# SSD output projection: seven products of quarters instead of eight, with the sums made by adding DMAs

## The chip, the cores and the metric

The kernel runs on one core of one Trainium2 chip. The metric is the device time of one execution in microseconds (us); less is better. The engines are TensorE (PE for its matmuls, PEld for its weight loads), VectorE (DVE), ScalarE (ACT), GpSimd (POOL) and SyncE (SP, which here only issues DMAs). Each has its own queue and works it off in order; semaphores join them.

## What is computed

One hybrid decoder layer on 1024 tokens of width 1024, in float32. Cut to what matters:

```python
h = rms_norm(x, norm_mix_g)
z, xbc, dt_raw, q_a, kv_a, k_rope_raw, gates = split(h @ w_in)
y_ssd = ssd_mixer(z, xbc, dt_raw, ...) @ w_ssd_proj     # (1024 x 2048) @ (2048 x 1024): the changed product
y_mla = mla_mixer(q_a, kv_a, k_rope_raw, ...) @ w_mla_proj
g_ssd, g_mla = split(sigmoid(gates + gate_b))
x = x + (g_ssd * y_ssd + g_mla * y_mla) @ w_o           # the merge, and w_o
h = rms_norm(x, norm_ffn_g)
x = x + ffn(h)                                          # gated MLP with a causal convolution

def ssd_mixer(z, xbc, dt_raw, ...):                     # state space scan: 4 groups of 8 heads, 8 chunks of 128 tokens
    xbc = silu(causal_depthwise_conv(xbc))
    y = ssd_chunked_scan(...) + xs * d_skip
    y = y * silu(z)
    return rms_norm(y in 4 groups of 512, norm_g)
```

## The kernel before

Activations lie with channels on the partitions and tokens along the row: a tile is 128 channels x 512 tokens (half the sequence). Precision is kept by splitting every operand in a high and a low part (`hi` is a rounding cast on ACT, `lo` the remainder on DVE or POOL); one step of a product is then three matmuls (`mm3`): hi x hi, hi x lo, lo x hi.

**The scan.** `ssd_steps(g)` goes through the 8 chunks of group g. Per chunk: transposes and scores on PE (tiles `xp`, `sp`), DVE's `sm`, `xdt`, `xde`, `bt`, `seg`, `abc` made from them, the new state (`sn` on PE, then `st`: multiplied by `cdec` on POOL, summed on DVE), and the output (`yp` on PE, added and gated on DVE into `xg`). Between these steps PE takes matmuls of other projections from a list, `background`: `conv_group(g + 1)`, which projects and convolves the next group's channels, `z_tiles`, and for the last group `mla_tiles`. Their tile is `lin`. `conv_group` gives way (`yield False`) as long as `finished[0] < g - 1`. `ssd_finish(g, half)` norms one half of a group: sums of squares and a Newton root on small tiles (`grr`, `rsa`), transposes into `np_`, four products on DVE (L957), and a store into `y_d` (L965). It is resumed a piece at a time from the loop over the next group, and its last act for half 1 is to set `finished[0]`.

**The projection.** The first half's y is split into `ya0` (from `y_d`, or directly for the last group). Then for each half and each of 8 column tiles, 16 tiles of k are multiplied into one PSUM bank: 8 x 2 x 16 x 3 = 768 matmuls of 128x512. The first of the 16 outputs begins inside the scan's last part (`first_ssd_tile`, the head). Behind each output come gates `gt` and the MLA part `mt` (loaded by POOL's queue) and the merge: (gt + 1) * y + mt, then half of it is split into `m`, all with DVE and ACT. Weights are loaded by SP in pieces of 256 KB into two buffers `wraw`, cast by ACT and subtracted by DVE (`whi`, `wlo`).

**w_o.** When the 8 merged tiles of a half are there, w_o follows, on top of x, loaded in one DMA of 2 MB per half into `x2` (L1240), then the FFN. Order: projection half 0, w_o half 0, projection half 1, w_o half 1. A framework orders each engine's queue by its own model of the program; in some stretches the order written in the code is kept.

Of the kernel before, what the change touches and what calls it, by code (L numbers as in the profile page):

```python
# [9 lines left out]
F32 = mybir.dt.float32  # L10
# [62 lines left out]
def tile_hybrid_layer(ctx: ExitStack, tc: tile.TileContext, x, cols, cons, w_main, w_small, w_uq, w_ukv,  # L73
# [15 lines left out]
    y_d = dram.tile([2 * D, T], F32, name="y_d")  # L89
# [83 lines left out]
    def mm3(ps, a, b, first, last, **more):  # L173
        (ah, al), (bh, bl) = a, b
        PE.matmul(ps, lhsT=ah, rhs=bh, start=first, stop=False, **more)  # L175
        PE.matmul(ps, lhsT=ah, rhs=bl, start=False, stop=False, **more)  # L176
        PE.matmul(ps, lhsT=al, rhs=bh, start=False, stop=last, **more)  # L177

# [163 lines left out]
    with tc.tile_pool(name="ap", bufs=2) as apool, tc.tile_pool(name="bls", bufs=4, space=PSUM) as bls:  # L342
# [48 lines left out]
        for half in range(2):  # L391
# [380 lines left out]
    with tc.tile_pool(name="dp", bufs=2) as dp, tc.tile_pool(name="psx", bufs=1, space=PSUM) as psx, \  # L772
# [166 lines left out]
        def ssd_finish(g, half):  # L939
# [16 lines left out]
            for j in range(4):  # L956
# [3 lines left out]
                if g == GROUPS - 1 and half == 0:  # L960
# [3 lines left out]
                else:  # L964
                    nc.sync.dma_start(out=y_d[r0:r0 + P, s], in_=x[:, j, s])  # L965
            if half:
# [27 lines left out]
        def mla_tiles():  # L994
# [11 lines left out]
            def y_step(j):  # L1006
# [5 lines left out]
                if j < 24 and j % 2 == 0:  # L1012
# [4 lines left out]
                    staged.append(raw_load(y_d, k, hs_(0), raw))  # L1017
# [34 lines left out]
        def first_ssd_tile():  # L1052
            ws = [load_w(w_ssd[0, kp], [P, KD, P]) for kp in range(2)]
            ps = lin_tile()
            head.append(ps)
            for k in range(16):
                while ya0[k] is None:
                    yield False
                hi, lo = ws[k // KD]
                mm3(ps, (hi[:, k % KD, :], lo[:, k % KD, :]), (ya0[k][:, 0, :], ya0[k][:, 1, :]), k == 0, k == 15)  # L1060
                yield True
# [40 lines left out]
        background.append(first_ssd_tile())  # L1102
# [70 lines left out]
    with tc.tile_pool(name="ep", bufs=2) as ep:  # L1173
        x2b = []
        with tc.tile_pool(name="em", bufs=2) as em:
# [32 lines left out]
            m0 = [em.tile([P, 2, 512], F32R, name="ma", bufs=3) for _ in range(3)]  # L1208
            for half in range(2):
                if half:  # L1210
                    w_raw(q0, loaded)
                    w_raw(q1, loaded)
                s = hs_(half)
                ya = ya0 if half == 0 else [load_act(y_d, k * P, s) for k in range(16)]
                ms = []
                for ct in range(8):
                    gt = em.tile([P, 512], F32, name="gt")
                    nc.gpsimd.dma_start(out=gt, in_=g_d[ct * P:(ct + 1) * P, s])
                    mt = em.tile([P, 512], F32, name="mt")
                    nc.gpsimd.dma_start(out=mt, in_=m_d[ct * P:(ct + 1) * P, s])  # L1220
                    if half == 0 and ct == 0:
                        ps = head[0]
                    else:
                        ps = lin_tile()
                        drain([steps([load_w(w_ssd[ct, kp], [P, KD, P]) for kp in range(2)], ya, ps, range(16), 16)])
                    if ct == 5:
                        loaded = last(mybir.EngineType.SP)
                    V.scalar_tensor_tensor(gt, gt, 1.0, ps, op0=ALU.add, op1=ALU.mult)
                    V.tensor_tensor(gt, gt, mt, op=ALU.add)  # L1229
                    m = em.tile([P, 2, 512], F32R, name="m", bufs=5) if ct >= 3 else \  # L1230
                        em.tile([P, 2, 512], F32R, name="ma", bufs=3) if half else m0[ct]
                    S.mul(m[:, 0, :], gt, 0.5)
                    V.scalar_tensor_tensor(m[:, 1, :], gt, 0.5, m[:, 0, :].bitcast(F32), op0=ALU.mult, op1=ALU.subtract)
                    ms.append(m)
                if half:
                    x0 = [x2b[0][:, i, :] for i in range(4)]
                    drain([norm(x0, x0, ep, x2ss[0])])
                big = ep.tile([P, 4, D], F32, name="x2")
                x2b.append(big)
                nc.sync.dma_start(out=big, in_=x[s, :].rearrange("(i p) c -> p i c", p=P))  # L1240
                behind(loaded)
                sq4 = ep.tile([P, 4, 2], F32, name="sq4")
                x2ss.append(sq4)
                nq = 0
                for ch in range(2):
                    banks = [bank6() for _ in range(4)]
                    qs = slice(ch * 512, (ch + 1) * 512)
                    for kp in range(4):
# [8 lines left out]
                        if half and (ch, kp) in ((1, 0), (1, 1)):  # L1257
                            q = pairs[kp]
                            q.a = w_split(q.r1, hp_tiles(), V)
                            w_sums(q, act_tile().rearrange("p a (b c) -> p (a b) c", c=P).bitcast(F32) if kp else None)  # L1260
                        if half and (ch, kp) == (1, 3):
# [5 lines left out]
                        for i in range(4):  # L1267
                            tk = slice(i * P, (i + 1) * P)
                            for k in range(2):
                                m = ms[2 * kp + k]  # L1270
                                mm3(banks[i], (m[:, 0, tk], m[:, 1, tk]), (wh[:, k, :], wl[:, k, :]),
                                    kp == 0 and k == 0, kp == 3 and k == 1)
                            if kp == 3:
                                V.tensor_tensor(big[:, i, qs], banks[i], big[:, i, qs], op=ALU.add)
                                junk = em.tile([P, 512], F32, name="junk", bufs=1)
# [4 lines left out]
                            if half and i % 2 and nq < KD:  # L1280
# [504 lines left out]
    for n, ins in enumerate(nc.cur_bb.bb.instructions):  # L1785
        if ins.engine == mybir.EngineType.PE or \
                (n < start_end or strict <= n < strict_end or n >= ordered) and ins.engine != mybir.EngineType.SP:
# [87 lines left out]
```

## Time and profile before

| | |
|---|---|
| runs (three) | 2176.78, 2179.0, 2181.62 us; median 2179.0 |
| profiled execution | 2178.96 us, its span 2177.1 us |
| granted TensorE clock, mean | 0.999 |
| POOL, share of the span | 41% |
| moved by DMA | 269.50 MB, mean 124 GB/s |
| scan with projections beside it | about 880 to 1260 us |
| projection half 0, then w_o half 0 | about 1260 to 1348, then from 1348 us |

The profile is of one execution. A busy PE is not PE at its peak: matmuls overlap, so the distance between starts tells more than a duration. In rows of groups, the idle time named is that of the engine just before the group's instructions, with what ended most of it.

### The profile page before, as it was taken

How to read it: one execution, taken by the hardware profiler on the slowest of the kernel's cores; microseconds unless marked ns; L12 is line 12 of the kernel's file. 1: busy time of each engine (PE TensorE's matmuls, PEld its weight loads, DVE VectorE, ACT ScalarE, POOL GpSimd, SP SyncE). 2: the span in 40 equal slices, each digit the busy share in tenths (PEclk: the TensorE clock that was granted, in tenths of full speed). 3: DMA queues.
4: the chain of work that ended last, by engine and by line, in shares of the span. 5: the costliest groups of instructions: out<-in, count | busy, mean ns of one | idle time of the engine just before them, and what ended most of it. 6: DMA issues, size and time to landing. Idle time of an engine off the chain costs nothing.

```text
span 2177.1 us, 30390 instructions
## 1 busy us (share of the span) xinstructions
PE 2136.6 (98%) x10844; PEld 1708.5 (78%) x10844; DVE 1445.6 (66%) x2613; ACT 1063.4 (49%) x2032; POOL 885.1 (41%) x1001
## 2 busy tenths in 40 slices
PE   8999999999999999999999999999999999999999
PEld 7877777777777887777878887888778888888887
DVE  4566656575665369898877755645786666677873
ACT  5445544555454446565654423324655554454441
POOL 2344424432542237665546411003098787750000
PEclk9999999999999999999999999999999999999999
DMA  4221111111211324645366557453132232348852
GB/s 149 70 68 43 44 55 58 52 40 55 65 40 64 121 75 137 193 155 179 105 203 208 167 193 252 163 189 102 63 121 100 99 101 98 112 150 315 275 188 83
DMA packets 121912, 269.50 MB, mean 124 GB/s; under 512 B 13536, under 2 KB 25760, under 8 KB 121760
## 3 DMA queue, kind: packets, MB, share of 16 engines
q1 hardware_dynamic: 105744, 214.99, 29.6%
q0 software_dynamic: 14528, 49.29, 6.7%
q10 hardware_dynamic: 1488, 3.28, 0.4%
q8 instruction: 85, 1.39, 0.3%
q14 instruction: 67, 0.55, 0.1%
HBM read 201.97 MB, written 65.54 MB: 123 GB/s over the span
## 4 chain that ended last, share of the span: by engine, by line
PE 75%; DVE 13%; ACT 5%; DMA 4%; issue 2%; POOL 1%; SPq 0%; ACTq 0%; DVEq 0%; POOLq 0%
PE lin L175 14%; PE lin L177 14%; PE lin L176 13%; PE dps L176 6%; PE dps L175 6%; PE dps L177 6%; PE pv L670 3%; PE s L175 2%; PE s L176 2%; PE s L177 2%; DVE xg L812 1%; PE s L627 1%; DMA wraw<-in_w_ssd 1%; PE yp L891 1%; PE s L610 1%
## 5 line engine op out<-in xcount | busy, mean ns | idle before, releaser
L175 PE MATMUL lin<-h,whi 128*128 128x512 f32 x1440 | 592.4, 411 | 2.2 <-DVE lt L330 2.2
L177 PE MATMUL lin<-h,wlo 128*128 128x512 f32 x1440 | 563.9, 392 | 0.0
L176 PE MATMUL lin<-h,whi 128*128 128x512 f32 x1440 | 562.9, 391 | 0.0
L175 PEld LDWEIGHTS lin<-h,whi 128*128 128x128 f32 x1440 | 271.0, 188 | 84.8 <-issue 33.8
L177 PEld LDWEIGHTS lin<-h,wlo 128*128 128x128 f32 x1440 | 270.6, 188 | 59.7
L176 PEld LDWEIGHTS lin<-h,whi 128*128 128x128 f32 x1440 | 271.7, 189 | 53.4 <-issue 7.0
L153 ACT CAST whi<-wraw 128x512 fp32r<-128x512 f32 x232 | 140.9, 619 | 260.7 <-PE lin L176 114.6
L154 POOL TENSOR_TENSOR wlo<-wraw,whi 128x512 fp32r<-128x512 f32 x134 | 193.4, 1460 | 171.1 <-ACT whi L153 167.6
L664 POOL TENSOR_TENSOR acc<-acc,e 128x512 f32<-128x512 f32 (+3 forms) x80 | 78.8, 985 | 245.1 <-ACT e L659 223.3
L659 ACT ACTIVATE e<-s 128x512 f32<-128x512 f32 (+1 forms) x192 | 93.4, 492 | 152.3 <-DVE s L657 131.2
L1140 DVE TENSOR_TENSOR xlo<-ur,xhi 128x512 fp32r<-128x512 f32 (+1 forms) x40 | 80.3, 2007 | 57.7 <-ACT xhi L1139 57.7
L154 DVE TENSOR_TENSOR wlo<-wraw,whi 128x512 fp32r<-128x512 f32 x98 | 69.6, 724 | 73.6 <-ACT whi L153 73.4
L850 ACT ACTIVATE seg<-abc,acum 128x128 f32<-128x128 f32 x256 | 80.1, 390 | 47.9 <-PE yp L891 41.8
L175 PE MATMUL dps<-tq,h 128*128 128x512 f32 x242 | 95.6, 395 | 0.0
L176 PE MATMUL dps<-tq,h 128*128 128x512 f32 x242 | 95.5, 395 | 0.0
L177 PE MATMUL dps<-tq,h 128*128 128x512 f32 x242 | 95.5, 394 | 0.0
L812 DVE SCALAR_TENSOR_TENSOR xg<-craw,cl,xg 128x1024 f32<-128x1024 f32 x48 | 73.8, 1536 | 27.4 <-ACT xg L810 26.9
L664 DVE TENSOR_TENSOR acc<-acc,e 128x512 f32<-128x512 f32 (+3 forms) x80 | 55.0, 687 | 37.9 <-ACT e L659 37.3
L670 PE MATMUL pv<-e,vt 128*64 128x512 f32 (+3 forms) x384 | 72.9, 498 | 0.0
L629 DVE CUSTOM_DVE_ANT_0 s<-s,negw 128x128 f32<-128x128 f32 (+3 forms) x128 | 62.3, 495 | 13.7 <-PE s L627 13.6
L175 PE MATMUL s<-qh,kh 97*128 97x512 f32 (+1 forms) x192 | 68.6, 357 | 1.3 <-ACT qh L644 0.9
L1220 POOL DMA_DIRECT2D mt<-m_d x16 | 8.6, 540 | 144.3 <-DVE gt L1229 96.0
(640 smaller groups left out, 5118.4 us busy)
## 6 DMA issues: line engine op xcount, KB each, us to landing
wraw<-in_w_main SPq DMA_DIRECT2D x112, 256.0 KB
ur<-in_w_up SPq DMA_DIRECT2D x43, 512.0 KB
abc<-ac_d POOLq DMA_DIRECT2D x32, 512.0 KB, 5.4
wraw<-in_w_ssd SPq DMA_DIRECT2D x64, 256.0 KB
ar<-f_d SPq DMA_DIRECT2D x32, 512.0 KB
g_d<-lt SPq DMA_DIRECT2D x32, 256.0 KB
z_d<-lt SPq DMA_DIRECT2D x32, 256.0 KB
zt<-z_d POOLq DMA_DIRECT2D x32, 256.0 KB, 3.4
```

The source lines that it names most:

```text
L153: S.copy(hi, raw)
L154: (eng or V).tensor_sub(lo, raw, hi.bitcast(F32))
L175: PE.matmul(ps, lhsT=ah, rhs=bh, start=first, stop=False, **more)
L176: PE.matmul(ps, lhsT=ah, rhs=bl, start=False, stop=False, **more)
L177: PE.matmul(ps, lhsT=al, rhs=bh, start=False, stop=last, **more)
L629: V.tensor_tensor_reduce(ps[:, 0:w], ps[:, 0:w], negw[:, 512 - w:512], 1.0, 2 * NEG, ALU.add, ALU.max, nm[:, j, i:i + 1])
L659: S.activation(e[:, c0:512], ps[:, 0:w], AF.Exp)
L664: (V if hd else G).tensor_tensor(accs[hd][:, c0:512], accs[hd][:, c0:512], e[:, c0:512], op=ALU.add)
L670: PE.matmul(pv[hd * 64:(hd + 1) * 64, c0:512], lhsT=vt[:, j, hd * 64:(hd + 1) * 64], rhs=es[hd][:, c0:512], start=first, stop=last)
L812: V.scalar_tensor_tensor(c, raw[:, k:k + T], col(cw + k), c, op0=ALU.mult, op1=ALU.add)
L850: S.activation(seg[:, hd, :], abc[:, hd, :], AF.Relu, bias=acum[:, c, 8 * g + hd:8 * g + hd + 1], scale=-1.0)
L1140: eng.tensor_sub(lo, r, hi.bitcast(F32))
```

## The change

The 2048 x 1024 weights and the 2048 x 1024 activations are each seen as 2 x 2 quarters: `h` is the half of k (of every group of four tiles the first or the second two), and the column tiles 0 to 3 and 4 to 7, and the two halves of the sequence. Seven products of quarters, in the form of Strassen and Winograd, replace eight. Each product is 4 units (column tiles) of 8 steps: 7 x 4 x 8 x 3 = 672 matmuls. The sums of quarters that products need are made by DMAs that add into their destination (`accum_op=ALU.add`), which only POOL's queue issues; to make differences, the norm's gain of half of the channels is negated, and a split can turn a sign (`minus`).

- Activations: `ssd_finish` stores its normed halves in tensors `t_d` (s1 to s4 and 22), plain by SP, and adds into them by POOL. Its generator gets two more yields for half 0 and one more for half 1.
- Weights: `raw_q` loads them plain by SP and adds by POOL, into `e1` (the `x2` buffer of the pool `ep`, 2 MB) or `ur`.
- The products are worked in the order 1, 2, 3, 7, 6, 5, 4; `finish_unit` adds the results on DVE and makes the merged tiles. Two units of product 1 are the new head (`first_products`).
- Both halves' projections now come ahead of w_o. The gates of the second half are merged within w_o's first half. Gates are loaded by SP. Both x loads stand after the last product.
- In the stretch of the products every engine's queue but SP's keeps the written order.

The diff, cut:

```diff
+    def quarter_split(raws, minus=False):
+        ...
+            if minus:
+                S.mul(h, raw, -1.0)
+                V.scalar_tensor_tensor(l, raw, -1.0, h.bitcast(F32), op0=ALU.mult, op1=ALU.subtract)
+            else:
+                split(raw, h, l)
 ...
+    def quarter_step(ps, w, t, kk, first):
+        mm3(ps, (w[0][:, kk, :], w[1][:, kk, :]), (t[:, 0, :], t[:, 1, :]), first and kk == 0, kk == KD - 1,
+            skip_group_check=True)
 ...
+                minus = cl[:, CG_SSDG:CG_SSDG + 16].rearrange("p (g j) -> p g j", j=4)[:, :, 2:4]
+                G.tensor_scalar(minus, minus, -1.0, None, op0=ALU.mult)
 ...
+                elif half == 0:
+                    nc.sync.dma_start(out=y_d[r0:r0 + P, :], in_=x[:, j, s])
+
+            def form(v, *names, **more):
+                for n in names:
+                    (nc.gpsimd if more else nc.sync).dma_start(
+                        out=t_d[n][2 * g * P:2 * (g + 1) * P, :].rearrange("(j p) t -> p j t", p=P), in_=v, **more)
+
+            a1, a2 = x[:, 0:2, s], x[:, 2:4, s]
+            if half == 0:
+                form(a1, "s2", "s3", "s4")
+                yield
+                yield
+                form(a2, "s4", accum_op=ALU.add)
+            else:
+                form(a1, "s1")
+                form(a2, "22")
+                form(a1, "s3", "s2", "s4", accum_op=ALU.add)
+                yield
+                form(a2, "s1", "s2", "s4", accum_op=ALU.add)
                 finished[0] = g + 1
             yield
 ...
+            def raw_q(t, ct, h, **more):
+                for kp in range(2):
+                    (nc.gpsimd if more else nc.sync).dma_start(
+                        out=t[:, 4 * kp:4 * kp + 4, :].rearrange("p (g j) c -> p g (j c)", j=2),
+                        in_=quarter_w(ct, h, kp), **more)
 ...
+            units = [(p, i) for p in (1, 2, 3, 7, 6, 5, 4) for i in range(4)]
+            source = {3: "s4", 7: "s3", 6: "s2", 5: "s1", 4: "22"}
+            following = {2: 3, 3: 7, 7: 6, 6: 5, 5: 4}
 ...
+            for n in range(2, len(units)):
+                p, i = units[n]
+                weights(n + 1)
+                weights_raw(n + 2)
+                while fresh:
+                    forms[following[units[n - 1][0]]].append(ordered_split(fresh.pop(0)))
+                if p in following:
+                    v = t_d[source[following[p]]]
+                    for k in ((0, 1, 2), (3, 4, 5), (6, 7), ())[i]:
+                        fresh.append(raw_load(v, k, slice(0, 512), lt.tile([P, 512], F32, name="lt")))
+                if p == 2:
+                    raw_q(e1[:, i], i + 4, 1)
+                    raw_q(e1[:, i], i + 4, 0, **plus)
+                elif p == 7:
+                    raw_q(ur[i], i + 4, 0)
+                    raw_q(ur[i], i, 0, **plus)
+                if p in (3, 4):
+                    gm[i] = gates(i if p == 3 else 4 + i, 0)
+                ...
+                for kk in range(KD):
+                    quarter_step(b, ws[p, i], forms[p][kk], kk, p in (1, 2, 3, 7))
+                finish_unit(p, i)
+            bigs = [ep.tile([P, 4, D], F32, name="x2") for _ in range(2)]
             for half in range(2):
+                nc.sync.dma_start(out=bigs[half], in_=x[hs_(half), :].rearrange("(i p) c -> p i c", p=P))
 ...
+                        if not half:
+                            c = us[n_][:, ch, :]
+                            gated(gates(n_ if ch else n_ + 4, 1), c, mr[n_] if ch else c, ch == 1)
```

How it moves instructions, at three places. First PE's queue in group 1's scan, near its second and third chunk. A number behind a name tells buffers apart. Before, one scan step, then projection matmuls:

```order
L874 MATMUL sn_9518<-xde_9443,bt_9445 128x512
L175 MATMUL lin_9459<-h_595,whi_9373 128x512
...
L177 MATMUL lin_9546<-h_282,wlo_9537 128x512
L840 MATMUL xp_9568<-cn_81,xg_8441 128x128 x4
L842 MATMUL sp_9573<-chan_8302,chan_8169 128x128
...
L175 MATMUL lin_9546<-h_307,whi_9536 128x512
...
L891 MATMUL yp_9609<-seg_9431,xdt_9441 64x128 x2
...
L175 MATMUL lin_9636<-h_458,whi_9536 128x512
...
L874 MATMUL sn_9652<-xde_9590,bt_9592 128x512
```

After, with the two chunks in one piece, and the transposes of the norm (`np_`) in it:

```order
L909 MATMUL sn_9515<-xde_9433,bt_9435 128x512
L176 MATMUL lin_9449<-h_601,whi_9359 128x512
...
L875 MATMUL xp_9541<-cn_86,xg_8447 128x128 x4
...
L926 MATMUL yp_9570<-seg_9421,xdt_9431 64x128 x2
...
L990 MATMUL np__9594<-cn_86,grr_9464 128x128 x4
L909 MATMUL sn_9608<-xde_9563,bt_9565 128x512
L875 MATMUL xp_9626<-cn_86,xg_8447 128x128 x4
...
L926 MATMUL yp_9658<-seg_9551,xdt_9561 64x128 x2
...
L176 MATMUL lin_9693<-h_221,whi_9683 128x512
...
L909 MATMUL sn_9706<-xde_9648,bt_9650 128x512
```

Before, 12 to 15 matmuls of `lin` stand between any two scan steps here; after, there are none from xp_9541 to yp_9658, then 12. The same is found in group 2. The matmuls taken out stand at the group's end: 72 of `lin` in one piece in group 1, 144 in group 2.

Second, PE's queue at the head of the projection, where the last norm's transposes stand. Before:

```order
L177 MATMUL lin_12728<-h_12662,wlo_12709 128x512
L955 MATMUL np__12753<-cn_81,grr_12688 128x128 x4
L175 MATMUL lin_12728<-h_12668,whi_12718 128x512
...
L177 MATMUL lin_12728<-h_12458,wlo_12719 128x512
L175 MATMUL lin_12820<-h_12435,whi_12821 128x512
```

After:

```order
L178 MATMUL lin_12787<-h_12480,wlo_12733 128x512
L990 MATMUL np__12812<-cn_86,grr_12772 128x128 x4
L176 MATMUL dps_12858<-h_12465,whi_12866 128x512
L177 MATMUL dps_12858<-h_12465,whi_12866 128x512
L178 MATMUL dps_12858<-h_12465,wlo_12867 128x512
```

and DVE's queue there, after:

```order
L992 SCALAR_TENSOR_TENSOR xg_10759<-xg_10759,cl_85,np__12812 128x512 x4
L155 TENSOR_TENSOR wlo_12867<-wraw_12862,whi_12866 128x512
L155 TENSOR_TENSOR wlo_12867<-wraw_12863,whi_12866 128x512
```

Eight steps (24 matmuls) of the first output stood between the transposes and the next output's weights `wlo`; now the third matmul after the transposes needs a `wlo` that DVE makes behind the four products of the norm.

Third, SP's queue at the start of w_o. Before, x is loaded 12 DMAs ahead of w_o's first weights:

```order
L1240 DMA x2_13360<-in_x 128x4x1024
L160 DMA wraw_13211<-in_w_ssd 128x512
...
L160 DMA wraw_13303<-in_w_ssd 128x512
L1253 DMA wraw_13369<-in_w_o 128x2x256
```

After, both loads of x stand between the first weights of w_o, which come far earlier, and its second:

```order
L1372 DMA x2_14012<-in_x 128x4x1024
L1262 DMA gt_14021<-g_d_82 128x512
L1264 DMA mt_14023<-m_d_83 128x512
L1372 DMA x2_14013<-in_x 128x4x1024
L1262 DMA gt_14061<-g_d_82 128x512
L1264 DMA mt_14063<-m_d_83 128x512
L1398 DMA wraw_14069<-in_w_o 128x2x256
L1398 DMA wraw_14073<-in_w_o 128x2x256
```

The second pair of weight pieces for w_o is behind 5 MB of loads on this queue.

More of the change, by code (lines that the diff above doesn't have):

```diff
@@ L959, in ssd_finish @@
                 r0 = (4 * g + j) * P
-                if g == GROUPS - 1 and half == 0:
+                if half == 0 and g == GROUPS - 1:
                     t = act_tile()
@@ L1214, in tile_hybrid_layer @@
[L1214 to L1234, printed above, removed]
@@ L1235, in tile_hybrid_layer @@
-                if half:
+                    m12 = [merged(mr[i], em.tile([P, 2, 512], F32R, name="mu", bufs=4)) for i in range(4)]
+                    ms = m12 + m22
                     x0 = [x2b[0][:, i, :] for i in range(4)]
-                    drain([norm(x0, x0, ep, x2ss[0])])
-                big = ep.tile([P, 4, D], F32, name="x2")
+                    drain([norm(x0, x0, ep, x2ss[0], group=4)])
+                big = bigs[half]
                 x2b.append(big)
-                nc.sync.dma_start(out=big, in_=x[s, :].rearrange("(i p) c -> p i c", p=P))
```

158 lines of the change are left out of this document (127 added, 31 removed).

## The prediction

> **What bounds the kernel now.** I read the page first; this is its busy time by engine.
>
> ```profile
> PE 2136.6 (98%) x10844; PEld 1708.5 (78%) x10844; DVE 1445.6 (66%) x2613; ACT 1063.4 (49%) x2032; POOL 885.1 (41%) x1001
> ```
>
> TensorE is busy for 98% of the span, so a matmul taken away is worth its own time, if the work beside it keeps up. A busy PE does not tell the price of one matmul, since neighbours overlap. So next the timeline of PE inside the SSD projection (columns: start, duration, engine, line, operation), and a window of 20 us (PE busy and its instructions, granted clock, DMA share, GB/s).
>
> ```profile
> 1279.83 0.39 PE L176 MATMUL lin<-h,whi 128*128 128x512 f32 x1
> ...
> 1281.42 0.39 PE L177 MATMUL lin<-h,wlo 128*128 128x512 f32 x1
> 1280.00:1300.00 20.00, 20.00 (x89) 1.00 0.51 158
> ```
>
> Between those two starts lie seven steps: (1281.42 - 1279.83) / 7 = 0.227 us from start to start, though each row lasts 0.39. I use 0.228. The clock is full.
>
> Then the waits of PE (time in total, times, longest) from 800 to 1262 us, where the SSD scan runs with projections between its matmuls, and of PE in the projection and the first half of w_o after it:
>
> ```profile
> PE sn L874 <- DVE bt L863: 4.4, 3, 2.3
> PE lin L175 <- DVE lt L330: 2.2, 1, 2.2
> PE np__12753 L955 <- DVE grr L125: 1.3, 1, 1.3
> PE yp L891 <- DVE seg L864: 0.8, 2, 0.5
> PE dps L176 <- DVE wlo L154: 1.1, 3, 0.6
> ```
>
> There is under 10 us of idle PE to win here, and none in the projection itself; what can be lost is larger. From 880 to 1040 us the window (length, then busy time of PE, PEld, DVE, ACT, POOL) shows why:
>
> ```profile
> 880.00:1040.00 160.00, 157.05 (x978) 125.89 (x976) 143.88 (x218) 97.17 (x185) 99.12 (x86) 1.00 0.52 168
> ```
>
> VectorE is busy for 143.88 of 160 us. The scan hides only because projection matmuls stand between its steps.
>
> **The change part by part.**
>
> *Products.* Before: 8 column tiles x 2 halves x 16 tiles of k x 3 = 768 matmuls; after: 7 products x 4 units x 8 x 3 = 672. 96 fewer, at 0.228: **-21.9 us**.
>
> *The scan loses its cover in groups 1 and 2.* `ssd_finish` yields more often, so it sets `finished[0]` later, and `conv_group`, which waits for that, holds back the projections. In the new order PE has, from the first sn of group 1's stretch: 3 lin, xp and sp, yp, np, sn, xp and sp, yp, 12 lin, sn. Before, 12 to 18 lin stood between each two of these. The held matmuls run at the group's end beside no scan. What PE does in that piece, by rows of before (each step is the time to the next start):
>
> ```profile
> 928.10 1.02 PE L874 MATMUL sn<-xde,bt 128*128 128x512 f32 x2
> 928.56 0.79 PE L175 MATMUL lin<-h,whi 128*128 128x512 f32 x1
> ...
> 932.41 0.60 PE L840 MATMUL xp<-cn,xg 128*128 128x128 f32 x4
> ...
> 933.09 0.48 PE L175 MATMUL lin<-h,whi 128*128 128x512 f32 x1
> ...
> 936.02 0.44 PE L891 MATMUL yp<-seg,xdt 128*64 128x128 f32 x4
> ...
> 937.92 0.50 PE L175 MATMUL lin<-h,whi 128*128 128x512 f32 x1
> ```
>
> sn 0.46, xp with sp 0.68, yp 1.90; np, from rows below, 0.37. PE's piece is 15 x 0.228 + 2 x 0.68 + 2 x 1.90 + 0.37 + 0.46 = 9.4 us. DVE must meanwhile go from st to the bt of that last sn:
>
> ```profile
> 932.23 0.68 DVE L881 TENSOR_TENSOR st<-st,sn 128x512 f32<-128x512 f32 x1
> 933.42 1.22 DVE L867 TENSOR_TENSOR abc<-abc,chan 128x1024 f32<-128x1024 f32 x1
> 937.61 0.28 DVE L847 SCALAR_TENSOR_TENSOR sm__9576<-sp,cn 128x128 f32<-128x128 f32 x1
> 939.01 0.68 DVE L855 TENSOR_TENSOR xdt<-xp,dtt 128x512 f32<-128x512 f32 x1
> 941.24 0.68 DVE L860 TENSOR_TENSOR xde<-xp,dte 128x512 f32<-128x512 f32 x1
> 941.84 0.27 DVE L863 COPY bt<-sp 128x128 f32<-128x128 f32 x1
> 942.04 1.26 DVE L864 TENSOR_TENSOR seg<-seg,sm__9576 128x1024 f32<-128x1024 f32 x1
> 931.19 1.11 DVE L903 SCALAR_TENSOR_TENSOR xg<-xg,hds,yp 128x128 f32<-128x128 f32 x4
> 932.82 0.68 DVE L905 SCALAR_TENSOR_TENSOR xg<-zt,xg 128x512 f32<-128x512 f32 x1
> 928.56 2.71 DVE L957 SCALAR_TENSOR_TENSOR xg<-xg,cl,np__9469 128x512 f32<-128x512 f32 x4
> L812 DVE SCALAR_TENSOR_TENSOR xg<-craw,cl,xg 128x1024 f32<-128x1024 f32 x28 | 42.9, 1530 | 11.1 <-ACT xg L810 10.9
> 1259.76 0.16 DVE L125 SCALAR_TENSOR_TENSOR grr<-rsa,grr 128x4 f32<-128x4 f32 x1
> ```
>
> Two chunks' sm, xdt, xde, bt: 2 x 1.91 = 3.8; two st 1.4; abc 1.2; seg 1.3; yp added and gated 1.8; norm 2.7; three steps of the convolution 3 x 1.53 = 4.6; three small ones 0.5. That is 17.3 us against 9.4: **+8 us**. Group 2 has the same list (17.1) against PE's 9.4 + 9 more lin, 11.5: **+5 us** after rounding down, since some of the conv steps may be done early. Low end 4 in all (the new order gives DVE only what before it also had, and it had 16 us of 160 free); high end 24, if each of the two handovers per chunk waits once more for DVE's whole queue (16 and 8).
>
> *Adding DMAs on POOL's queue.* Seven stores of 512 KB per group stand on GpSimd's queue, two of them behind an earlier one into the same tensor, and the next state's multiply is queued behind these. Before has no adding DMA. Nearest rows: a 512 KB load of that queue (KB, median us to landing), the issue of one, and that multiply:
>
> ```profile
> abc<-ac_d POOLq DMA_DIRECT2D x32, 512.0 KB, 5.4
> 926.36 0.59 POOL L788 DMA_DIRECT2D abc<-ac_d  x1
> 925.37 1.05 POOL L879 TENSOR_TENSOR st<-st,cdec 128x512 f32<-128x512 f32 x1 [3.40 <-PE yp L896]
> ```
>
> Seven issues take 4.1 us and one wait 5.4, against 3.40 us in which POOL stood idle ahead of the multiply, and the multiply's result is only needed behind the next sn, some 5 us on. At the plain price this is hidden: **0**; at three times it is 16 - 8 = 8 late in one group. I take the plain price, by the nearest row. Range 0 to 8. The Trainium skill, "DMA: Bandwidth & Descriptors", in its rules for authors, says that an accumulating DMA must wait for the semaphore of an earlier one into the same bytes; the new order has just these waits, and no run here shows their length.
>
> *Head of the projection.* Before, eight steps of projection follow the last transposes of the norm and cover what DVE does behind them:
>
> ```profile
> 1260.07 0.62 PE L955 MATMUL np__12753<-cn,grr 128*128 128x128 f32 x4 [1.34 <-DVE grr L125]
> 1260.44 0.48 PE L175 MATMUL lin<-h,whi 128*128 128x512 f32 x1
> ...
> 1260.73 2.72 DVE L957 SCALAR_TENSOR_TENSOR xg<-xg,cl,np__12753 128x512 f32<-128x512 f32 x4 [0.81 <-PE np__12753 L955]
> 1263.37 1.29 DVE L154 TENSOR_TENSOR wlo<-wraw,whi 128x512 fp32r<-128x512 f32 x2
> ```
>
> After, the transposes stand right ahead of the unit whose wlo is split behind the norm on DVE. The first half of that wlo is there 0.66 + 2.64 + 0.65 = 3.9 us after the transposes start; PE wants it after 0.37 + 2 x 0.228 = 0.8: **+3.1 us**. The sums, 1.34 us of waiting here, stay.
>
> *Second product.* Its plain and adding loads of weights begin by waiting for every adding store of group 3, on SP's queue, with weight loads behind them; 8.4 MB (four times 2 MB of forms, weights and additions) move in 4 x 5.5 = 22 us, some 380 GB/s, where the projection now takes 158. **+0.5 us**, from 0 to 5 (one weight load of the row above, landing late).
>
> *Products 3 to 4.* At most six DVE operations of about 0.69 per unit and a few on ACT, against 24 x 0.228 = 5.5 us of PE: 0. Forms and weights are fetched a product ahead.
>
> *Start of w_o.* Before, the 2 MB of x were loaded in two parts, each inside the projection. Their effect on the weight loads behind shows at the second (SP's issue, then ACT's cast, then the window):
>
> ```profile
> 1440.37 0.43 SPq L1240 DMA_DIRECT2D x<-in_x  x1
> 1444.08 7.91 SPq L160 DMA_DIRECT2D wraw<-in_w_ssd  x3
> 1450.29 0.62 ACT L153 CAST whi<-wraw 128x512 fp32r<-128x512 f32 x1 [4.97 <-DMA wraw<-in_w_ssd]
> 1440.00:1450.00 10.00, 10.00 (x45) 8.29 (x45) 3.19 (x5) 1.77 (x3) 1.08 (x2) 1.00 0.93 348
> ```
>
> 9.9 us lie between the issue of x and the cast of the weights behind it, with the DMA engines 93% busy. After, both loads of 2 MB stand on SP's queue between the last product's gates and the second pair of weight tiles of w_o, which is needed 5.5 us after w_o begins and, by 9.9 us, is split at about 10: +4.6, less the 1.1 us that PE waits there now: **+3.5 us**, from -1 to +8. A rule speaks against the relief of moving the adding loads to another queue: by the Trainium skill, "DMA: Bandwidth & Descriptors", section "Issuing engines are not separate DMA queues", transfers of all issuers share the same engines and interleave. The last row agrees (0.93 of all sixteen, from SP and POOL together); by a rule of separate queues this term would be 0 and the sum 3.5 us lower.
>
> *Waits that go.* At the head of group 3 ACT's queue stood behind a late weight load, and lin after lt (2.2) and the longest sn wait (2.3) followed from it:
>
> ```profile
> 1133.86 0.62 ACT L153 CAST whi<-wraw 128x512 fp32r<-128x512 f32 x1 [3.59 <-DMA wraw<-in_w_mla]
> ```
>
> In the new order six tiles run unbroken ahead of it, so I take the first and half of the second: **-3.2 us**, from 0 to -4.5. Half 1's sixteen loads and splits of y hung on no wait that PE shows: 0. Later stages: 0.
>
> **Sum**: -21.9 + 8 + 5 + 0 + 3.1 + 0.5 + 3.5 - 3.2 = -5.0 us. The profiled execution took 2178.96 us, 0.04 under the median of the runs (2179.0), so both give **2174.0 us**. A difference under 0.2% (4.4 us) is no difference that can be measured.
>
> **The rivals.**
> 1. *The scan stays covered.* DVE works ahead while PE does the 66 to 72 displaced matmuls; the two stalls are 4 us in all and x is early enough: -21.9 + 4 + 3.1 + 0.5 + 1 - 3.2 = -16.5, **2162.5 us**. For it: PE waits on bt and seg only 5.2 us in all now. Against it: the order lets nothing of a chunk begin before its xp.
> 2. *The scan is bare, slower.* At groups 1 and 2 each handover between PE and DVE waits: 16 + 8, and the waits at group 3 stay: -21.9 + 24 + 3.1 + 0.5 + 3.5 = +9.2, **2188 us**. It decides from 15 us on at these two places. For it: VectorE's 90%. Against: waits of 2.3 at most today.
> 3. *Adding transfers are dear.* At three times a plain one, POOL holds the state in groups 1 and 2 (half of 8 each) and the second product starves by 5: -5 + 8 + 4.5 = +7.5, **2186.5 us**. For it: a sum has to be read before it is written. Against: no row. The change then does not do what it says: the DMAs don't add for nothing.
>
> **How the numbers follow.** Likeliest (0.42): 2174.0, itself from 2168 to 2181. Rival 1: 0.25; rival 2: 0.20; rival 3: 0.13. The range of 2161 to 2190 leaves out the lower third of rival 1 and the upper third of 2 and 3, near 2 in 10. Faster by over 0.2% (under 2174.6): rival 1 and about half of the likeliest, 0.47. Within: most of the rest of the likeliest, 0.20. Slower: rivals 2 and 3, 0.33.
>
> **What would show it.** PE instructions in the projection down by 96 and its stage at 0.228 a matmul; PE waits of about 8 and 5 us on bt and seg in groups 1 and 2; one of 3 us ahead of the first dps; one of 3 to 5 us on wlo soon after w_o begins; the multiply of st on POOL not late. I am wrong if PE's idle time in the scan stays under 6 us or passes 20, or if lines of the products wait for forms or weights.

## The result, and the profile after

| | before | after |
|---|---|---|
| median | 2179.44 us (4 runs, 2176.78 to 2181.62) | 2267.06 us (4 runs, 2265.86 to 2271.44) |
| ratio, 95% interval | | 1.0406 [1.0388, 1.0425] |
| profiled execution, its span | 2178.96, 2177.1 us | 2271.44, 2269.7 us |
| last transposes of the norm (end of the scan) start at | 1260.07 us | 1313.29 us |
| last matmul of w_o's second half starts at | 1522.62 us | 1612.81 us |

The change made the kernel 4.1% slower; 2174.0 us was predicted, with a range up to 2190. The page after (busy time, chain, queues with packets, MB and share of 16 DMA engines):

```profile
PE 2146.2 (95%) x10748; PEld 1707.9 (75%) x10748; DVE 1478.5 (65%) x2593; ACT 1075.5 (47%) x2048; POOL 930.9 (41%) x1030
PE 63%; DVE 15%; DMA 9%; ACT 5%; issue 4%; POOL 3%; SPq 0%; ACTq 0%; POOLq 0%; DVEq 0%
q0 software_dynamic: 28288, 63.97, 11.4%
t_ds<-xg POOLq DMA_DIRECT2D x28, 512.0 KB, 8.9
```

The 96 matmuls are gone (10844 to 10748), yet PE is busy 10 us longer and idle for some 80 us more. The longest waits of PE after, from 800 to 1620 us (time in total, times, longest):

```profile
PE dps L176 <- ACT whi L154: 49.0, 7, 24.9
PE sn L909 <- DVE bt L898: 14.5, 5, 4.4
PE xp L875 <- DVE xg L852: 7.9, 1, 7.9
PE lin L176 <- ACT craw L843: 5.2, 2, 4.7
PE lin L176 <- DVE chan L1085: 4.4, 1, 4.4
PE yp L926 <- DVE seg L899: 4.0, 4, 2.0
```

The first line is the products' stage and w_o, the others are the scan. Up to the last transposes 53.2 us were lost; 24 more matmuls stand ahead of them (5.5 us), so the scan is 47.7 us longer. From there to w_o's end another 37.0 were lost, though 120 matmuls fewer stand there.

That PE is busy longer with fewer matmuls is the clock. The trace has the granted clock at 0.50 in stretches of 3.41 us or multiples of it; PE was busy in 60.6 us of these, before the change in 3.4. At half speed that is 30 us lost against 2. After the longest wait (start, duration):

```profile
1338.83 0.79 PE L176 MATMUL dps<-h,whi 128*128 128x512 f32 x1 [24.93 <-ACT whi L154]
1339.42 0.63 PE L177 MATMUL dps<-h,whi 128*128 128x512 f32 x1
...
1343.26 0.39 PE L177 MATMUL dps<-h,whi 128*128 128x512 f32 x1
1343.49 0.39 PE L178 MATMUL dps<-h,wlo 128*128 128x512 f32 x1
```

From 1339.42 to 1343.26 lie nine steps of 0.427 us, not 0.228: 1.8 us lost behind one wait. From 800 to 1620 us ten waits of 3.4 us or more, and two shorter ones, have such a stretch behind them.

What ended the wait of 24.93 us stands on ACT's queue, and behind it on GpSimd's:

```profile
1337.18 1.07 ACT L1322 COPY mu<-lin 128x512 f32<-128x512 f32 x2 [29.29 <-DMA t_ds<-xg]
1338.14 1.15 ACT L154 CAST whi<-wraw 128x512 fp32r<-128x512 f32 x2
1315.64 4.93 POOL L1004 DMA_DIRECT2D t_ds<-xg  x4 [17.46 <-DVE xg L992]
1326.45 1.20 POOL L1004 DMA_DIRECT2D t_ds<-xg  x1 [5.88 <-DMA t_ds<-xg]
1328.75 1.20 POOL L1004 DMA_DIRECT2D t_ds<-xg  x1 [1.10 <-DMA t_ds<-xg]
```

The copy of product 1 goes into `mu`, whose memory was the last group's `xg`. It can't be written before the last adding store has read it, 20 us after the norm; the cast of the next weights is queued behind the copy.

The second place is product 3. DVE waits for the gates, ACT for DVE, PE for ACT's cast:

```profile
1385.53 0.89 SPq L1262 DMA_DIRECT2D gt<-g_d  x1
1393.16 0.69 DVE L1275 SCALAR_TENSOR_TENSOR gt<-gt,mu 128x512 f32<-128x512 f32 x1 [9.93 <-DMA gt<-g_d]
1394.62 0.63 ACT L1269 ACTIVATE ma<-mu 128x512 fp32r<-128x512 f32 x1 [11.62 <-DVE mu L1279]
1395.15 1.12 ACT L154 CAST whi<-wraw 128x512 fp32r<-128x512 f32 x2
1395.81 0.79 PE L176 MATMUL dps<-h,whi 128*128 128x512 f32 x1 [7.87 <-ACT whi L154]
```

256 KB took 7.6 us from issue to use, behind adding loads of weights; before, `gt` landed 4.1 us after its issue (median). PE waited 2.1, 7.9 and 3.5 us in product 3 and 4.6 ahead of the next one, product 7. The third place is the one that was predicted, the start of w_o:

```profile
1522.00 0.80 PE L176 MATMUL dps<-whi,ma 128*128 128x512 f32 x1 [5.66 <-ACT whi L154]
```

### The profile page after: what moved, and what is told of

The parts are those of the page before. It is cut to its first block, busy times and chain, and to the rows that moved or that the text cites. A ratio compares the mean times of both kernels' runs of the same rounds, so it can differ in the third digit from the quotient of the medians.

```text
span 2269.7 us, 30297 instructions
## 1 busy us (share of the span) xinstructions
PE 2146.2 (95%) x10748; PEld 1707.9 (75%) x10748; DVE 1478.5 (65%) x2593; ACT 1075.5 (47%) x2048; POOL 930.9 (41%) x1030
## 3 DMA queue, kind: packets, MB, share of 16 engines
q0 software_dynamic: 28288, 63.97, 11.4%
## 4 chain that ended last, share of the span: by engine, by line
PE 63%; DVE 15%; DMA 9%; ACT 5%; issue 4%; POOL 3%; SPq 0%; ACTq 0%; POOLq 0%; DVEq 0%
PE lin L176 10%; PE lin L178 10%; PE lin L177 10%; PE dps L176 7%; PE dps L178 7%; PE dps L177 7%; DMA t_ds<-xg 4%; PE pv L705 2%; DVE xg L847 2%; PE s L176 2%; PE s L177 2%; PE s L178 2%; PE s L662 1%; PE s L645 1%; POOL wlo L155 1%
## 5 line engine op out<-in xcount | busy, mean ns | idle before, releaser
L176 PE MATMUL lin<-h,whi 128*128 128x512 f32 x1232 | 514.4, 418 | 10.8 <-ACT craw L843 5.2
L178 PE MATMUL lin<-h,wlo 128*128 128x512 f32 x1232 | 486.1, 395 | 0.3 <-POOL wlo L155 0.2
L177 PE MATMUL lin<-h,whi 128*128 128x512 f32 x1232 | 484.7, 393 | 0.0
L176 PEld LDWEIGHTS lin<-h,whi 128*128 128x128 f32 x1232 | 233.8, 190 | 86.6 <-issue 38.5
L178 PEld LDWEIGHTS lin<-h,wlo 128*128 128x128 f32 x1232 | 233.2, 189 | 54.4 <-POOL wlo L155 1.5
L177 PEld LDWEIGHTS lin<-h,whi 128*128 128x128 f32 x1232 | 234.6, 190 | 46.1 <-issue 7.1
L154 ACT CAST whi<-wraw 128x512 fp32r<-128x512 f32 x184 | 111.6, 619 | 191.3 <-PE lin L177 61.5
L176 PE MATMUL dps<-h,whi 128*128 128x512 f32 x260 | 105.4, 405 | 43.0 <-ACT whi L154 43.0
L178 PE MATMUL dps<-h,wlo 128*128 128x512 f32 x260 | 105.2, 405 | 0.6 <-DVE wlo L155 0.6
L177 PE MATMUL dps<-h,whi 128*128 128x512 f32 x260 | 104.4, 402 | 0.0
L176 PEld LDWEIGHTS dps<-h,whi 128*128 128x128 f32 x260 | 51.1, 196 | 55.6 <-ACT whi L154 45.3
```

The costliest lines, as they stand in the source:

```text
L154: S.copy(hi, raw)
```

## The experiments

Times are medians of four runs (ten of the run without sums of activations), ratios are to runs of the kernel before on the same chip (its medians were 2177.2 to 2179.9).

### What the scan pays for

**Yields alone**, on the kernel before:

```diff
-            if half:
+            if half == 0:
+                yield
+                yield
+            else:
+                yield
                 finished[0] = g + 1
```

> The kernel before with nothing changed but the three added yields in ssd_finish (two in half 0, one in half 1), so that finished is set as late as in the changed kernel. Theory (the scan lost its cover by the late flag): most of the 47 us that the changed kernel lost up to the head comes back here, so 2205 to 2225 us, with waits of sn on bt and of xp on xg in groups 1 to 3. Rival (the scan is slow because of the adding stores on POOL's queue and their traffic): within 10 us of before, 2175 to 2190.

Measured: 2202.37 us, 1.0102 [1.0087, 1.0118], 22.5 us over before. The waits are those of the changed kernel, at the same places:

```profile
937.61 2.08 PE L874 MATMUL sn<-xde,bt 128*128 128x512 f32 x2 [4.06 <-DVE bt L863]
1020.73 0.47 PE L840 MATMUL xp<-cn,xg 128*128 128x128 f32 x1 [4.35 <-DVE xg L817]
1074.94 2.07 PE L874 MATMUL sn<-xde,bt 128*128 128x512 f32 x2 [4.43 <-DVE bt L863]
1285.10 0.60 PE L955 MATMUL np__12777<-cn,grr 128*128 128x128 f32 x4
```

The last row is the yardstick from here on: the transposes that end the scan start at 1285.1, in the changed kernel at 1313.3. That is 25.0 us later than before, 19.5 without the 24 matmuls that now stand ahead of them. So the late flag is a cost, of 19.5 of the scan's 47.7 us; neither theory alone was right. Up to the transposes PE is idle 12.6 us longer than before (21.3 against 8.7 from 860 us on), and busy 6.9 us longer than the 24 matmuls account for; that is the clock (18.4 us of busy time at half speed in this run, 3.4 before).

**No adding stores.** All `form(..., accum_op=ALU.add)` left out (so the sums of activations are not made), yields kept.

> The changed kernel with the seven adding stores per group left out (the tensors then hold only the plain part); yields, plain stores and the adding loads of weights stay. Theory of the late flag: the scan stays slow (the last np transposes near 1305 us or later), only the 24.9 us wait at product 1 goes with its slow clock behind it, so 2235 to 2245 us. Rival (adding stores): the scan also recovers 30 to 45 us, so 2190 to 2205.

Measured: 2223.27 us, 1.02 [1.0185, 1.0215]; transposes at 1285.23. It lies between the two: the adding stores cost 28 us of the scan on top of the flag's part, and another 16 behind it. There PE's wait at product 1 is 7.50 us in this run, against 24.93.

Three runs then asked what it is about them, with every store going to a tensor of its own, so that the sums are left out.

```diff
-                form(a2, "s4", accum_op=ALU.add)
+                form(a2, "b4", accum_op=ALU.add)     # and so on: no two into one tensor
```

> The changed kernel with each adding store going to a tensor of its own (the sums then stay apart, part of the computation is left out), so that the same adding DMAs move the same bytes and none waits for an earlier one into the same tensor. Theory (GpSimd's queue is held by those waits, 53.7 us in the changed kernel, and abc, zt, st and gate loads behind it come late): most of the 28 us that the adding stores cost in the scan come back, and some of the wait at product 1: 2225 to 2240 us. Rival (the adding itself takes the DMA engines' time): at most 10 us back, 2257 or more.

Measured: 2261.83 us, 1.0386 [1.037, 1.0401]; transposes at 1307.85. The theory of held waits fell: taking the waits away gives 5.4 of the 28 us.

```diff
-                form(a2, "s4", accum_op=ALU.add)
+                form(a2, "b4")                       # and so on: plain, by SP
```

> The changed kernel with the same seven stores per group as plain stores on SP's queue into tensors of their own (the sums are left out): same bytes written, nothing on GpSimd's queue, nothing added. Theory (hold of GpSimd's queue, or price of the adding): close to the run without them, 2220 to 2232 us. Rival (bytes stored beside the scan): 2240 or more.

Measured: 2232.63 us, 1.0253 [1.0238, 1.0269]; transposes at 1285.21. The bytes alone cost the scan nothing. They are not free behind it: PE waits 15.94 us at product 1, 8.4 more than without the stores, since the copy into `mu` has to wait for plain stores too.

```diff
-                    (nc.gpsimd if more else nc.sync).dma_start(..., in_=v, **more)
+                    (nc.gpsimd if more else nc.sync).dma_start(..., in_=v)    # plain, still by POOL
```

> The changed kernel with the same seven stores per group still issued by GpSimd, but as plain stores into tensors of their own (the sums are left out). Plain stores on SP's queue gave the last np transposes at 1285.2 us, adding stores without waits 1307.9, with waits 1313.3. Theory (the adding itself is what the scan pays for): as on SP, transposes at 1283 to 1288, 2228 to 2238 us. Rival (GpSimd's time to issue them, 28 times 1.2 to 1.5 us, holds what is queued behind): transposes at 1300 or later, 2248 us or more.

Measured: 2235.19 us, 1.0259 [1.0243, 1.0274]. The end of the scan, plain by POOL:

```profile
1288.98 0.60 PE L991 MATMUL np__12819<-cn,grr 128*128 128x128 f32 x4
```

and adding, without waits:

```profile
1307.85 0.60 PE L991 MATMUL np__12819<-cn,grr 128*128 128x128 f32 x4
```

So of 28.1 us, POOL's issuing of plain stores costs 3.8, making them adding ones 18.9, the waits between them 5.4. It is the transfer that is slow, not the issue: six adding stores, issued one right behind another from 1310.85 to 1314.54 us, landed from 1317.9 to 1330.9, one every 2.6 us; six plain ones, issued from 1292.62 to 1296.24, landed from 1296.9 to 1304.0, one every 1.4.

More than half of the 18.9 can be followed in the traces. The next group but one is convolved into the `xg` that the stores still read. ACT's first write there, in group 2's scan, plain, then adding without waits, then the changed kernel:

```profile
1091.62 1.24 ACT L846 ACTIVATE xg<-craw,cl 128x1024 f32<-128x1024 f32 x1
1105.08 1.24 ACT L846 ACTIVATE xg<-craw,cl 128x1024 f32<-128x1024 f32 x1 [6.20 <-DMA wraw<-in_w_main]
1104.95 1.25 ACT L845 ACTIVATE xg<-craw,cl 128x1024 f32<-128x1024 f32 x1 [6.68 <-DMA t_ds<-xg]
```

In the changed kernel the trace names the store. In the second row it names a load, but the group's last adding store, issued at 1090.41, landed 14.5 us later, at 1104.9, just ahead of ACT; the last plain one landed at 1089.3 and held nobody. The first such write, in group 1's scan, waited 2.83 us in the adding run, until 976.1, where the last store landed at 975.9. DVE then waited 3.39 us for ACT, with the scan's next steps behind it on its queue, and PE 5.04 us for `bt`. By the starts of `sn`, the adding run falls behind the plain one by 4.3 us at the first place and by 6.1 at the second. The other 8.5 us are not traced.

The queue tables agree that adding is dear (packets, MB, share of 16 engines). Without the seven stores:

```profile
q1 hardware_dynamic: 118608, 229.67, 30.9%
q0 software_dynamic: 20672, 49.29, 7.8%
```

With them plain by SP:

```profile
q1 hardware_dynamic: 126224, 244.36, 32.1%
```

With them plain by POOL:

```profile
q0 software_dynamic: 24704, 63.97, 9.5%
```

The same 14.7 MB took 32.1% of 2229.1 - 30.9% of 2222.4 = 28.8 us of all sixteen engines when SP stored them, 9.5% of 2232.5 - 7.8% of 2222.4 = 38.8 when POOL did, and 11.4% of 2269.7 - 173.3 = 85.4 when they were added: 3.0 times the first and 2.2 times the second.

**No yields**, adding stores kept (the three added `yield` taken out of the changed kernel).

> The changed kernel without the three added yields, so that finished is set where it was before and the projections stand between the scan's steps again. Theory (the two costs of the scan add, 22.5 us by the late flag alone): 2240 to 2250 us. Rival (six adding stores now stand in one piece on GpSimd's queue, three waits in a row ahead of the state, and hold it longer): 2258 or more, with waits of PE on st or on what POOL loads.

Measured: 2253.09 us, 1.035 [1.0333, 1.0367], between the two: 14 us won of the 22.5. The scan ends at 1298.40, with 24 fewer matmuls ahead of that: 38 us later than before, and 33.4 later than in the run without sums below (1264.96), so the adding stores cost it more than with the yields. PE waits elsewhere:

```profile
PE lin L178 <- POOL wlo L155: 16.8, 4, 5.3
PE sn L909 <- DVE st L916: 5.6, 1, 5.6
```

The weight splits and the state's multiply on GpSimd's queue stand behind the stores: this is the hold that the prediction had priced at nothing. The changed kernel has it too, one engine further from PE. Up to the end of its scan, GpSimd's waits for an earlier store, and DVE's for the state's multiply (1.0 us before the change):

```profile
POOL t_ds L1004 <- DMA t_ds<-xg: 46.7, 9, 12.0
DVE st L916 <- POOL st L914: 22.0, 4, 8.1
```

### What the products' stage pays for

**Late copies.**

```diff
-                if p == 1:
-                    S.copy(c, X[i])
-                elif p == 2:
+                if p == 2:
+                    S.copy(c, X[i])
                     V.tensor_tensor(c, Z[i], c, op=ALU.add)
```

> The changed kernel with the four copies of product 1 into mu put at the end of the same unit of product 2, so that ACT's queue no longer stands at mu for the last adding stores (29.3 us there) ahead of its weight casts. Theory: the 24.9 us wait of PE goes, and a smaller one of 5 to 10 us appears in product 2, where SP's first e1 load still waits for the same stores with weight loads behind it: 2245 to 2255 us. Rival (that SP wait, or the late weights, ends as late as the copies did): 2262 or more.

Measured: 2250.67 us, 1.0331 [1.0315, 1.0346], 16.4 less. The 24.9 us are gone; what they had hidden shows, the wait behind the norm at the head that was predicted (3.1 us), and one of 3.5 between products 2 and 3, for weights that landed late (5 to 10 had been expected):

```profile
1316.18 0.77 PE L176 MATMUL dps<-h,whi 128*128 128x512 f32 x1 [4.24 <-DVE xg L992]
1356.59 0.50 PE L176 MATMUL dps<-h,whi 128*128 128x512 f32 x1 [3.50 <-ACT whi L154]
```

**Early gates.** `gates` of products 3 and 4 moved one unit up, ahead of `weights_raw`:

```diff
+                if n + 1 < len(units) and units[n + 1][0] in (3, 4):
+                    gp, gi = units[n + 1]
+                    gm[gi] = gates(gi if gp == 3 else 4 + gi, 0)
                 weights_raw(n + 2)
```

> The changed kernel with the gate loads of products 3 and 4 issued one unit earlier, ahead of that unit's weights and activations on SP's queue. Theory: the waits of product 3 (2.1, 7.9, 3.5 and 4.6 us, DVE's gt on its DMA) go with some 2 us of slow clock behind each of the longer ones: 2243 to 2252 us. Rival (DMA engines are full with the adding loads, so whatever is loaded there is late): at most 5 us less, 2261 or more, with the wait now at whi on its own DMA.

Measured: 2252.66 us, 1.0329 [1.0311, 1.0346], 14.4 less, as the theory had it but for its last 0.7 us. Of product 3's waits 4.79 and 1.42 us are left, the first for weights that landed late, which is the sign that the rival had named.

**No adding loads of weights** (all `raw_q(..., **plus)` left out, gates as they were).

> The changed kernel with the adding loads of weights (8.4 MB) left out, the plain ones kept: the sums of weights are left out. Theory (adding transfers take three times the DMA engines' time, so gates and weights of product 3 came late behind them): the waits of product 3 fall by at least half: 2248 to 2258 us. Rival (the gates are late by their place in SP's queue alone): 2261 to 2268.

Measured: 2258.71 us, 1.0362 [1.0345, 1.0379], 8.4 less: between the two, closer to the theory. The waits of product 3 and ahead of product 7 fall from 18.1 to 10.1 us, not by half. Both the place in the queue and the dear loads made the gates late.

**Three mends**: late copies, early gates, and the second load of x put at `ch == 1` of w_o's first half.

> The changed kernel with the late copies and the early gates together, and the second load of x put into w_o's first half. Theory (three separate waits): 2267 - 16.4 - 14.4 and some 5 us for w_o = 2228 to 2238 us. Rival (they hide one another, or the second x load only moves its collision to later weights of w_o): 2242 or more.

Measured: 2232.86 us, 1.0251 [1.0234, 1.0269]: they add (34.2 us less). The wait at the start of w_o falls from 5.66 to 1.03 us.

**Four mends**: these and no yields.

> Late copies, early gates, second x load later, and no added yields, all together. Theory (the gains add: 2232.9 with three of them, 14 us by the yields): 2214 to 2224 us. Rival (without the yields the adding stores stand in one piece and their end moves behind the head): 2228 or more.

Measured: 2223.72 us, 1.0207 [1.0192, 1.0223]. The yields are worth 9.1 us here, not 14, and the kernel is still 46 us over before.

### What the sums cost in any form

**Sums on GpSimd's arithmetic**, in place in `xg`, all stores plain, with the four mends:

```diff
+                G.tensor_tensor(a2, a2, a1, op=ALU.add)      # half 0
+                form(a2, "22")                               # half 1, b1 and b2 are half 0's a1 and a2
+                G.tensor_tensor(a2, a2, a1, op=ALU.add)
+                form(a2, "s1")
+                G.tensor_tensor(b2, b2, a2, op=ALU.add)
+                form(b2, "s4")
+                G.tensor_tensor(a1, a1, b1, op=ALU.add)
+                form(a1, "s3")
+                G.tensor_tensor(a2, a2, b1, op=ALU.add)
+                form(a2, "s2")
```

> As the run with four mends, but with no adding store at all: the sums of activations are made by GpSimd's arithmetic in place in xg (one 128x2x512 add in half 0, four in half 1 of each group) and then stored plainly by SP. Theory (adding stores and the late flag were the two costs of the scan, 28 and 22.5 us): the scan is again near its length before, and the products' saving shows in part: 2172 to 2192 us. Rival (the chain of adds and stores keeps xg busy, and the next group's convolution or GpSimd's queue waits for it): 2200 or more, with waits of ACT's xg on the stores.

Measured: 2205.77 us, 1.0123 [1.0106, 1.014]: 18 us better than the adding DMAs, and 27.0 late at the end of the scan (1287.09, as many matmuls ahead as before). By its time the rival held.

**No sums of activations**, then **no sums at all** (also no adding loads of weights), with the four mends:

```diff
             if half == 0:
                 form(a1, "s2", "s3", "s4")
             else:
                 form(a1, "s1")
                 form(a2, "22")
```

> Late copies, early gates, second x load later, no added yields, and no sums of activations (only plain stores; the sums are left out), sums of weights kept. Theory (the scan is then as before, and the products give their 21.9 us less what their stage still waits, 12 to 18 us with the slow clock): head transposes at 1260 to 1264 us, 2168 to 2180 us. Rival (the stage is bound by transfers and gives nothing): 2184 or more.

> As the run without sums of activations, and the adding loads of weights left out too. Theory (adding loads take 6.2 us of all DMA engines per MB, 52 us in this stage, and make what little is late there late): 3 to 8 us under the run with them. Rival (hidden by now): within 2 us of it.

Measured: 2174.27 us, 0.998 [0.997, 0.9989], and 2163.63 us, 0.9928 [0.9914, 0.9943]. The end of the scan and the first wait of PE behind it, without sums of activations:

```profile
1264.96 0.62 PE L990 MATMUL np__12765<-cn,grr 128*128 128x128 f32 x4 [0.71 <-DVE grr L126]
1311.84 0.50 PE L176 MATMUL dps<-h,whi 128*128 128x512 f32 x1 [2.69 <-ACT whi L154]
```

and without any sum, where no product waits, and w_o's start is the first that does:

```profile
1263.61 0.62 PE L990 MATMUL np__12765<-cn,grr 128*128 128x128 f32 x4 [0.68 <-DVE grr L126]
1428.70 0.49 PE L176 MATMUL dps<-whi,h 128*128 128x512 f32 x1 [0.81 <-ACT whi L154]
```

From the transposes to w_o's last matmul it was 262.6 us before; here 1517.32 - 1264.96 = 252.4, and 1504.63 - 1263.61 = 241.0. Without any sum the stage gives 21.5 of the 21.9 us that 96 matmuls are worth; the sums of weights take 11.3 of it back, over the 3 to 8 that were expected.

**The same arithmetic without waits for stores**: `b1 += a1` (s3), `a1 += a2` (s1), `b2 += b1`, `b2 += a2` (s4), `a2 += b1` (s2) in half 1, all on GpSimd; then the first two and the last on VectorE.

> As z1, with the five in-place additions of a group in an order in which none but the last writes over a tile whose store has just been issued; all on GpSimd. Theory (GpSimd's queue was held by waits for stores, 47 us in z1): the scan's loss of 27 us falls below 12: 2183 to 2195 us. Rival (GpSimd's own time, five times 2.6 us per group, is what is late): 2200 to 2208.

> As z2, with three of the five additions on VectorE (about 1.3 us each). Theory (GpSimd's queue is the tighter one in the scan): 3 to 8 us under z2, 2178 to 2190 us. Rival (VectorE, 90% busy in group 1, pays for it): no better than z2.

Measured: 2205.56 us, 1.0118 [1.0103, 1.0133], no better than with the waits, so its theory fell; and 2198.35 us, 1.0091 [1.0076, 1.0106], 7 us under it, as its theory had it, though not at its time. With the sums shared, DVE itself is late in group 1, and the scan ends 13.2 us after the run without sums:

```profile
951.42 2.07 PE L909 MATMUL sn<-xde,bt 128*128 128x512 f32 x2 [7.67 <-DVE bt L898]
1278.13 0.62 PE L990 MATMUL np__12777<-cn,grr 128*128 128x128 f32 x4 [0.79 <-DVE grr L126]
```

No version that makes all the sums beat the kernel before: the sums of activations cost 49.4 us as adding DMAs (2223.72 - 2174.27), 31.3 on GpSimd, 24.1 on GpSimd and VectorE, where the rest of the change is worth 4.

## Why the prediction was wrong

Point by point, predicted term and what was measured:

- *Products, -21.9*: right. 21.5 in the run without sums.
- *The scan loses its cover, +8 and +5, and -3.2 for waits that go*: right in mechanism and place (group 1's sn waits 4.06 and 1.8 us), too small: with the yields alone the scan is 19.5 us longer and the kernel 22.5, against a net 9.8. PE's idle time in it, 12.6 us more, is near that sum. Two things were left out. The displaced matmuls cover the convolution of the next group too, so its `xg` came late (4.35 us at the next group's first xp, 7.88 in the changed kernel); and behind long waits the clock is low, 6.9 us here. The high end of 24 would have held.
- *Adding DMAs on POOL's queue, 0 (0 to 8)*: this step failed. It took a plain load's 5.4 us for an adding store's 8.9 (median, up to 14.1 in the scan), took one wait on POOL's queue per group where there were nine in the scan (46.7 us), and asked only for the hold of one multiply. It gave as a sign that the multiply is not late; DVE waited 22.0 us for it. Shown: 28 us in the scan, of them 18.9 by making the stores adding ones. The third rival had the price right (three times, measured 3.0 to plain stores by SP) and its consequence too small: it asked what was queued behind on POOL, not whose memory a store still reads. The wait for `xg` is the path of 10.4 of the 18.9 us; what the rest is, late loads or something else, is not shown.
- *Head, +3.1*: there, 4.24 us, once its cover is taken away. In the changed kernel it lies inside a wait of 24.9 us that the prediction does not have. It named one waiter for group 3's adding stores, SP's load into `e1`, and missed the other tile laid over the same memory, `mu`, and that ACT's casts are queued behind it.
- *Second product, +0.5*: 3.50 us between products 2 and 3 once the copies are late, within its range of 0 to 5.
- *Products 3 to 4, 0*: failed. It counted engines' operations per unit and not the gates' way: issued in the same unit, behind weights and forms, and needed at its end by DVE and ACT, whose order is fixed. Issuing them a unit earlier gives 14.4 us back.
- *Start of w_o, +3.5*: 5.66 and 1.80 us of waits against 1.1 before, so +6.4; right in mechanism, within its range.

The Trainium skill, "DMA: Bandwidth & Descriptors", section "Issuing engines are not separate DMA queues", says that DMAs of all issuers interleave on the same engines. The runs agree, and the prediction used the rule for w_o alone, where it bore on product 3 as well: POOL's adding loads delay what SP loads there, and 10.6 us separate the runs with and without them.

## What to carry to other kernels

A sum made by a DMA is not free because no engine computes it: by these runs, price it at two to three times a plain transfer of the same bytes, on the engines that also bring everything else, before you take 1% of the matmuls away for it. When a buffer is used again, or a pool is closed and another opened over it, list every first writer into the memory of a tile whose last reader is slow, on every queue, and what stands behind that writer. A load that is consumed in an engine's fixed order is issued a unit ahead of it, and a generator that gates others' work by a flag is not given a yield without asking who stands still meanwhile.

## What the runs showed of the hardware

- An adding store of 512 KB landed after 8.9 us (median), without waits between them after 9.0 to 14.5 in three sets; a plain one by the same queue after 6.1 to 7.5. 14.7 MB of adding took 85.4 us of all sixteen engines, where plain stores took 28.8 (issued by SP) or 38.8 (by POOL). It was cut into more packets: 7616 against 4032 on that queue. Its issue lasted 1.2 us or more, a plain store's 0.7, but issues next to one another started 0.7 to 0.8 us apart in both. Issued so, six adding ones landed 2.6 us apart, six plain ones 1.4.
- The granted clock fell to 0.50 for 3.41 us or a multiple behind every wait of PE of 3.7 us or more in these runs' scans and products. Shorter waits went both ways: one of 1.56 us in the run without sums of activations (at 1326.57) had it, one of 2.13 in the changed kernel (at 1381.93) had not. In such a stretch 128x512 matmuls stood 0.427 us apart, then 0.228 again. The Trainium skill, "TensorE: Matmul & The Clock Gate", Part 1, has the array fall to half its clock after an idle window of about 3.4 us and give 426.7 ns for such a matmul then; the traces agree on the 0.427 us, and show the fall behind shorter waits as well. By the nine slow steps above, a wait of 4 us cost nearly 6 (an estimate).
